# Differential attention heads in a hybrid decoder layer: merging maxima and sums by tensor_reduce, leaving head outputs in PSUM until they are stored, and making the high halves on ScalarE

## The chip, the cores and the metric

The kernel runs on one core of a Trainium2 chip. A core has five engines that run side by side and meet only through semaphores: TensorE (PE, matmuls; its weight loads are listed apart as PEld), VectorE (DVE), ScalarE (ACT), GpSimd (POOL) and SyncE (SP), which here issues the DMAs. Matmul results land in PSUM, a small memory of eight banks; everything else is held in SBUF. Each engine works through its own instructions strictly in order, so an instruction that waits holds up all that stands behind it.

The metric is device time in microseconds (us) of one execution, lower is better. Three executions of the kernel before took 2918.4 us (median), 2916.21 and 2920.43 us.

## The reference, cut to what matters

One decoder layer, sequence 2048, width 1024, float32 in and out:

```
h    = rmsnorm(x)
proj = h @ w_in                    # q, k, v of both head groups
8 heads x 64:  stick-breaking attention (sigmoids and a running product)
4 heads:       differential attention, two 64-wide maps each, 128-wide values:
    s[m] = (q[m] @ k[m].T) / 8, causal;  p[m] = softmax(s[m]),  m = 0, 1
    a    = p[0] - lam * p[1]
    o    = rmsnorm(a @ v) * (1 - lambda_init)          # per head
x = x + concat(heads) @ w_o
x = x + (silu(h2 @ w_gate) * (h2 @ w_up)) @ w_down     # h2 = rmsnorm(x)
```

q and k of the differential heads are also RMS-normed per 64 columns and rotated (rotary embedding).

Float32 accuracy is got from float16 matmuls: each operand is split into a high half (the value rounded to float16) and a low half (the rest), and a product is three matmuls, high by high, high by low and low by high.

## The kernel before, in words

**Stages.** The norm of the input with the first projections; the four pairs of stick-breaking heads; the four differential heads (g = 4 to 7); the output projection; the FFN. Projections of the next heads and, in the last head, the output projection of the first half, are cut into pieces and put between the attention work as filler for TensorE.

**Differential heads.** `units_diff` goes through 16 blocks of 128 queries ("rows" of a head, i = 0 to 15). Row i sees L = (i+1)*128 keys, in chunks of up to 1024. A unit is one map m (1 first, then 0) and one chunk j. A row therefore has two units when i < 8 (n = 1 chunk) and four when i >= 8 (n = 2). Of a unit, `scores` puts q by k into one of three two-bank PSUM slots; `front` takes the row maximum on DVE (L863, recorded through the helper `big` at L178) and, for the second chunk, merges it with that of the first (L865); `main` computes the bias (ACT, L871) and the exponentials with their sum (ACT, L874), both from PSUM.

**After the last unit of a row**, its remaining steps are put on a tick clock, one tick per unit: `coefs` (sums of two chunks added, L893, then a reciprocal and a product), `mix` (p0 plus a coefficient times p1, DVE, L178), `high` (float16 copy `ah`: ACT at L915 for rows with two chunks, DVE at L917 for the others) and `low` (the rest `al`: DVE, or POOL at L925 for one chunk of the long rows), each followed by a DMA transpose into `wt` (SP, L292). Then `values` at tick 7+n (PE: `wt` by v, three matmuls per 128 keys, into a 128-column PSUM place `acc`), `copy` at 8+n (ACT: acc to SBUF tile `on`, L946; squares with their sum, L948), `power` at 9+n (POOL), `store_high` at 10+n (ACT, L961) and `store` at 11+n (DVE, L966, then a DMA transpose, L968, and one tick later a DMA to `mix_d`, L710).

**The order inside a tick** is fixed by the main loop at the end of the attention part: first "ev" work, then `front` of unit n+1, then untagged work (`store`, `copy`), then `main` of unit n, then "mid" work (`values`, evacuations of projections), then the rest ("hi" work and `mix`, `low`), then the scores of unit n+2 and a piece of filler.

**PSUM.** It is one tile of 8 banks of 512 columns. In the differential stage `place` gives z (scores) banks 0 to 5 and `pj` (filler projections) the first 256 columns of bank 6 or 7 in turn; `av1`, the place of `acc`, is 128 columns in the upper half of the bank that the last `pj` tile did not get. Ordering between engines is put in by the framework, which orders accesses to the same bank.

**Projections of the differential heads** (`project_diff`): q and k parts are evacuated by ACT to `st` (L589); v by DVE, high at L605, low at L606. The rotation (`squares` to `finish`) is spread over some nine ticks on POOL and DVE; at its end `high` makes float16 copies of q (DVE, L665) and k (ACT, L666), and `finish` copies q's high half once more (DVE, L679). The helper `halved` makes a high half on ACT (L508) and a low half on DVE (L509) of a PSUM place.

Of the kernel before, what the change touches and what calls it, by code (L numbers as in the profile page):

```python
# [64 lines left out]
def hybrid_layer_kernel(  # L65
# [159 lines left out]
    with ExitStack() as actx:  # L225
# [24 lines left out]
        def place(kind, w):  # L250
            if kind == "av1":

                turn[kind] = 128 - turn.get(kind, 0)
                n = turn[kind] + (3840 if turn["pj"] % 2 == 0 else 3328)
                return psum[:, n:n + w]
            ps = places[mode[0]][kind]
            n = turn[kind] = (turn.get(kind, -1) + 1) % len(ps)
            return psum[:, ps[n]:ps[n] + w]


# [302 lines left out]
        def project_diff(c, g):  # L563
# [17 lines left out]
            for j in range(4):  # L581
# [21 lines left out]
                def evac_v(j=j, ps=ps):  # L603
                    vh, vl = v[:, j - 1:j + 1, 0, :], v[:, j - 1:j + 1, 1, :]
                    nc.vector.tensor_scalar(vh, ps, OUT_SC, None, ALU.mult)  # L605
                    nc.vector.scalar_tensor_tensor(vl, ps, OUT_SC, vh, ALU.mult, ALU.subtract)  # L606
# [54 lines left out]
            def high():  # L661
# [3 lines left out]
                nc.vector.tensor_copy(r["nq"][:, :, :, 0, :], xq)  # L665
# [11 lines left out]
            def finish():  # L677
                nq, nq2 = r["nq"], halves(n3)
                nc.vector.tensor_copy(nq2[:, :, :, 1, :], nq[:, :, :, 0, :])  # L679
# [152 lines left out]
        def unit_diff(g, i, m, j, cx):  # L832
# [21 lines left out]
            def front():  # L854

                if m == 1 and j == 0:
                    cx["mx"] = small("mx", 4, bufs=3)
                    cx["nb"] = small("nb", 4, bufs=3)
                    cx["su"] = small("su", 4, bufs=3)
# [4 lines left out]
                if j > 0:  # L864
                    nc.vector.tensor_max(mx[:, m:m + 1], mx[:, jj:jj + 1], mx[:, m:m + 1])  # L865

            def main():
                mx, nb, su = cx["mx"], cx["nb"], cx["su"]
                jj = 2 * j + m
                if j == 0:  # L870
                    nc.scalar.activation(nb[:, m:m + 1], mx[:, m:m + 1], AF.Identity,  # L871
                                         scale=nds_sc, bias=lnk)
# [16 lines left out]
            def coefs():  # L889
                su, cf = cx["su"], cx["cf"]  # L890
                steps = []
                if n == 2:
                    steps.append(lambda: nc.vector.tensor_add(su[:, 0:2], su[:, 0:2], su[:, 2:4]))  # L893
                steps += [lambda: nc.vector.reciprocal(cf[:, 0:1], su[:, 1:2]),
                          lambda: nc.vector.tensor_scalar(cf[:, 1:2], cf[:, 0:1], su[:, 0:1], nlam,
                                                          ALU.mult, ALU.mult)]

                def eps():
                    nc.gpsimd.tensor_scalar(cf[:, 2:3], su[:, 0:1], su[:, 0:1], scl[g][:, 2:3],
# [10 lines left out]
            def high(jc):  # L910
# [3 lines left out]
                if n == 2:  # L914
                    nc.scalar.copy(wh, p0)  # L915
                else:
                    nc.vector.tensor_copy(wh, p0)  # L917
# [12 lines left out]
            def values():  # L930
                acc = cx["acc"] = place("av1", 128)
# [800 lines left out]
```

## Time and profile before

| | us |
|---|---|
| median of 3 executions | 2918.4 |
| lowest, highest | 2916.21, 2920.43 |
| the profiled execution: time, span of its core | 2919.95, 2918.2 |
| busy in the span: PE, DVE, ACT, POOL | 2559.5, 2321.2, 1537.5, 1460.1 |
| mean granted TensorE clock | 0.947 of full speed |

All durations come from the one profiled execution, counted in microseconds from the start of its span; the 1.75 us between its time and its span lie outside what the trace shows. A group in the profile is named by line, engine, operation and tiles (output <- inputs), with its count, busy time, mean in ns, and the idle time of the engine just before, with what ended it. L167 is the helper through which all matmuls go, and L178 the helper `big`; there the tiles tell which step it is.

### The profile page before, as it was taken

How to read it: one execution, taken by the hardware profiler on the slowest of the kernel's cores; microseconds unless marked ns; L12 is line 12 of the kernel's file. 1: busy time of each engine (PE TensorE's matmuls, PEld its weight loads, DVE VectorE, ACT ScalarE, POOL GpSimd, SP SyncE). 2: the span in 40 equal slices, each digit the busy share in tenths (PEclk: the TensorE clock that was granted, in tenths of full speed). 3: DMA queues.
4: the chain of work that ended last, by engine and by line, in shares of the span. 5: the costliest groups of instructions: out<-in, count | busy, mean ns of one | idle time of the engine just before them, and what ended most of it. 6: DMA issues, size and time to landing. Idle time of an engine off the chain costs nothing.

```text
span 2918.2 us, 50458 instructions
## 1 busy us (share of the span) xinstructions
PE 2559.5 (88%) x19628; PEld 1475.6 (51%) x19628; DVE 2321.2 (80%) x3639; ACT 1537.5 (53%) x2587; POOL 1460.1 (50%) x1131
## 2 busy tenths in 40 slices
PE   6868878888687787776998899999999999999999
PEld 4435444446576676665763344444444444444444
DVE  7787878878898899899747788889877776776776
ACT  5777777877555555555415454544443343343332
POOL 1344444546667577576115456555445454445442
PEclk9979989889798899988999999999999999999999
DMA  4466776776745565667866312221126422112111
GB/s 157 83 129 119 131 131 114 140 127 124 130 74 96 94 106 100 127 121 135 188 155 139 106 65 103 96 80 62 44 87 132 135 94 73 44 44 87 44 44 72
DMA packets 734240, 301.55 MB, mean 103 GB/s; under 512 B 618672, under 2 KB 713264, under 8 KB 734000
## 3 DMA queue, kind: packets, MB, share of 16 engines
q1 hardware_dynamic: 733856, 298.30, 45.6%
q8 instruction: 153, 2.51, 0.4%
q14 instruction: 87, 0.71, 0.1%
q0 software_dynamic: 144, 0.03, 0.0%
HBM read 127.34 MB, written 28.31 MB: 53 GB/s over the span
## 4 chain that ended last, share of the span: by engine, by line
PE 48%; DVE 22%; ACT 9%; DMA 7%; POOL 6%; issue 6%; SPq 1%; DVEq 0%; ACTq 0%; POOLq 0%
PE pw L167 33%; PE psum L167 15%; DMA wt<-wl 3%; DVE mx L178 2%; DVE fs L1316 2%; DVE wl L790 2%; DVE acc_a L1589 2%; DVE gp L761 2%; ACT be L756 2%; DVE pt L178 1%; ACT gp L757 1%; DVE hh L1368 1%; DVE be L764 1%; ACT wh L785 1%; ACT psum L758 1%
## 5 line engine op out<-in xcount | busy, mean ns | idle before, releaser
L167 PE MATMUL pw<-t,fs 128*128 128x512 f16 x3696 | 808.5, 381 | 13.3 <-ACT fs L1315 3.8
L167 PEld LDWEIGHTS <-fs 128*128 128x128 f16 x3696 | 360.5, 98 | 452.4 <-issue 13.9
L772 POOL TENSOR_TENSOR be<-be,gp 128x1024 f32<-128x1024 f32 (+1 forms) x160 | 323.1, 2019 | 363.6 <-DVE gp L769 177.7
L167 PE MATMUL pw<-acc_b,at 128*128 128x512 f16 x2112 | 465.5, 380 | 17.2 <-DVE cg L1514 6.3
L167 PE MATMUL psum<-k,q 64*128 64x512 f16 (+4 forms) x1600 | 293.0, 383 | 131.9 <-ACT pt L874 79.8
L167 PE MATMUL psum<-ws,h_hi 128*128 128x128 f16 x4096 | 378.9, 225 | 17.3 <-ACT psum L948 10.8
L167 PE MATMUL psum<-ws,h_lo 128*128 128x128 f16 x2048 | 367.7, 224 | 0.0
L167 PEld LDWEIGHTS <-h_hi 128*128 128x128 f16 x4096 | 328.8, 101 | 47.5 <-issue 35.4
L167 PEld LDWEIGHTS <-at 128*128 128x128 f16 x2112 | 206.1, 98 | 268.7 <-issue 24.9
L1517 POOL TENSOR_TENSOR cg<-cg,cu 128x512 f32<-128x512 f32 x88 | 111.9, 1272 | 360.9 <-ACT cg L1516 341.1
L1589 DVE SCALAR_TENSOR_TENSOR acc_a<-pw,isd,acc_a 128x512 f32<-128x512 f32 x352 | 248.6, 744 | 49.9 <-PE pw L167 49.5
L761 DVE TENSOR_TENSOR_SCAN gp<-gp,psum 128x256 f32<-128x256 f32 (+1 forms) x320 | 196.4, 655 | 114.8 <-ACT psum L758 112.9
L1315 ACT ACTIVATE fs<-acc_b,fst 128x512 f16<-128x512 f32 x264 | 175.9, 713 | 211.1 <-POOL acc_b L1304 145.1
L1316 DVE SCALAR_TENSOR_TENSOR fs<-acc_b,fst,fs 128x512 f16<-128x512 f32 x264 | 248.2, 980 | 34.0 <-ACT fs L1315 33.9
L1506 POOL TENSOR_TENSOR sc<-sc 128x512 f32<-128x512 f32 x132 | 219.3, 1678 | 88.9 <-ACT sc L1500 88.9
L167 PEld LDWEIGHTS <-q 64*128 64x128 f16 (+1 forms) x1600 | 95.8, 100 | 239.2 <-issue 116.4
L167 PE MATMUL psum<-wt,v 128*64 128x256 f16 x1728 | 138.8, 308 | 84.8 <-DMA wt<-wl 74.4
L1500 ACT COPY sc<-pw 128x512 f32<-128x512 f32 x176 | 100.1, 580 | 211.4 <-PE pw L167 185.2
L167 PEld LDWEIGHTS <-h_lo 128*128 128x128 f16 x2048 | 206.5, 101 | 0.0
L874 ACT ACTIVATE pt<-psum,nb,ds_sc 128x1024 f32<-128x1024 f32 (+4 forms) x192 | 182.8, 952 | 21.6 <-DVE pt L178 8.3
L178 DVE TENSOR_REDUCE mx<-psum 128x1 f32<-128x1024 f32 (+4 forms) x192 | 173.6, 904 | 22.3 <-PE psum L167 21.6
L790 DVE TENSOR_TENSOR wl<-be,wh 128x1024 f16<-128x1024 f32 (+1 forms) x160 | 186.8, 1168 | 0.9 <-DMA wt<-wl 0.8
(224 smaller groups left out, 4596.3 us busy)
## 6 DMA issues: line engine op xcount, KB each, us to landing
acc_b<-in_w_gate_dram SPq DMA_DIRECT2D x22, 1024.0 KB, 5.2
acc_b<-in_w_up_dram SPq DMA_DIRECT2D x22, 1024.0 KB, 7.5
acc_b<-in_w_down_dram SPq DMA_DIRECT2D x22, 1024.0 KB, 9.4
raw<-in_w_in_dram SPq DMA_DIRECT2D x24, 512.0 KB, 4.5
xt<-in_x_dram SPq DMA_DIRECT2D x16, 512.0 KB, 5.5
raw<-in_w_o_dram SPq DMA_DIRECT2D x16, 512.0 KB, 4.0
mt<-mix_d SPq DMA_DIRECT2D x32, 256.0 KB, 3.4
out_dram<-acc_a SPq DMA_DIRECT2D x16, 512.0 KB, 2.6
```

What stands on the lines that cost most here:

```text
L167: nc.tensor.matmul(ps, lhsT=lhsT, rhs=rhs, start=start, stop=stop)
L178: fn(*a, **k)
L761: nc.vector.tensor_tensor_scan(ga, ga, z[:, h, P:W][:, ::-1], 2.0 ** 14 if diag else cx[a][:, h, 0:1], ALU.mult, ALU.mult)
L772: nc.gpsimd.tensor_mul(b4, b4, gp[:, :, 1:P + 1].rearrange("p h (r n) -> p h r n", r=1).to_broadcast([128, 2, 2, P]))
L790: nc.vector.tensor_sub(wl, b2, u["wh"])
L874: nc.scalar.activation(pt, u["z"][:, 0:e - b], AF.Exp, scale=ds_sc, bias=nb[:, m:m + 1], accum_out=su[:, jj:jj + 1])
L1315: nc.scalar.activation(w[:, m, 0:4], src, AF.Copy, scale=sw)
L1316: nc.vector.scalar_tensor_tensor(w[:, m, 4:8], src, sw, w[:, m, 0:4], ALU.mult, ALU.subtract)
L1500: nc.scalar.copy(s[m], y[m])
L1506: nc.gpsimd.tensor_add(s[m], s[m], y[m])
L1517: nc.gpsimd.tensor_mul(g, g, u)
L1589: nc.vector.scalar_tensor_tensor(acc[:, i, hs], ps, pr.isd, acc[:, i, hs], ALU.mult, ALU.add)
```

## The change

Four edits, all in the differential heads:

- the merging of two chunks' maxima and of their sums is done by `tensor_reduce` over wider tiles `mx` and `su`, into columns of their own, where `tensor_max` and `tensor_add` worked in place;
- a head's output stays in PSUM: `copy` no longer copies it to SBUF (the squares are now written to the SBUF tile `on`, and only their sum is used), and `store_high` and `store` read `acc` in PSUM. A new function `out_place` gives the place: it keeps a list of outputs not yet stored and takes the 128 columns of the bank that are free; where neither is free it would evict one to SBUF. In the built program it never does so: no copy of an `acc` is in it;
- v's high half is made by `halved` on ACT; q's float16 copy and its second copy go from DVE to ACT;
- `ah` of rows with one chunk goes from DVE to ACT.

```diff
@@ place @@
-            if kind == "av1":
-                turn[kind] = 128 - turn.get(kind, 0)
-                n = turn[kind] + (3840 if turn["pj"] % 2 == 0 else 3328)
-                return psum[:, n:n + w]
+        outs = []
+        def out_place(cx):
+            b = 3840 if turn["pj"] % 2 == 0 else 3328
+            free = [n for n in (b, b + 128) if n not in [o[0] for o in outs]]
+            if not free:
+                o = next(o for o in outs if o[0] in (b, b + 128))
+                outs.remove(o)
+                on = onp.tile([128, 128], F32, tag="on", name="on")
+                nc.scalar.copy(on, o[1]["acc"])
+                o[1]["acc"] = on
+                free = [o[0]]
+            outs.append((free[0], cx))
+            return psum[:, free[0]:free[0] + 128]
@@ project_diff @@
                 def evac_v(j=j, ps=ps):
-                    vh, vl = v[:, j - 1:j + 1, 0, :], v[:, j - 1:j + 1, 1, :]
-                    nc.vector.tensor_scalar(vh, ps, OUT_SC, None, ALU.mult)
-                    nc.vector.scalar_tensor_tensor(vl, ps, OUT_SC, vh, ALU.mult, ALU.subtract)
+                    halved(ps, v[:, j - 1:j + 1, 0, :], v[:, j - 1:j + 1, 1, :])
...
-                nc.vector.tensor_copy(r["nq"][:, :, :, 0, :], xq)
+                nc.scalar.copy(r["nq"][:, :, :, 0, :], xq)
...
-                nc.vector.tensor_copy(nq2[:, :, :, 1, :], nq[:, :, :, 0, :])
+                nc.scalar.copy(nq2[:, :, :, 1, :], nq[:, :, :, 0, :])
@@ unit_diff @@
                 if j > 0:
-                    nc.vector.tensor_max(mx[:, m:m + 1], mx[:, jj:jj + 1], mx[:, m:m + 1])
+                    nc.vector.tensor_reduce(mx[:, 4 + m:5 + m], mx[:, m:4:2], axis=AX.X,
+                                            op=ALU.max)
...
                 if n == 2:
-                    steps.append(lambda: nc.vector.tensor_add(su[:, 0:2], su[:, 0:2], su[:, 2:4]))
+                    steps.append(lambda: nc.vector.tensor_reduce(
+                        su[:, 4:6], su[:, 0:4].rearrange("p (j m) -> p m j", m=2), axis=AX.X,
+                        op=ALU.add))
...
-                if n == 2:
-                    nc.scalar.copy(wh, p0)
-                else:
-                    nc.vector.tensor_copy(wh, p0)
+                nc.scalar.copy(wh, p0)
...
             def values():
-                acc = cx["acc"] = place("av1", 128)
+                acc = cx["acc"] = out_place(cx)
...
             def copy():
-                on = cx["on"] = onp.tile([128, 128], F32, tag="on", name="on")
-                nc.scalar.copy(on, cx["acc"])
+                on = onp.tile([128, 128], F32, tag="on", name="on")
                 ss = cx["ss"] = small("oss", bufs=4)
-                nc.scalar.activation(cx["acc"], cx["acc"], AF.Square, accum_out=ss)
+                nc.scalar.activation(on, cx["acc"], AF.Square, accum_out=ss)
...
             def store():
-                on, ss = cx["on"], cx["ss"]
+                on, ss = cx["acc"], cx["ss"]
...
+                outs[:] = [o for o in outs if o[1] is not cx]
```

**Where it moves instructions.** TensorE's instructions stand in the same order as before; what they wait for is different. At the start of `values` of row 12 in head 6 (the first matmul of `wt` by v into `acc`) TensorE's queue read before:

```order
L167 LDWEIGHTS h_lo
L167 MATMUL psum<-ws,h_lo 128x128
L167 LDWEIGHTS wt [waits DMAHW1_49]
L167 MATMUL psum<-v,wt 128x128 [waits Activation_49]
L167 LDWEIGHTS wt
L167 MATMUL psum<-v,wt 128x128
```

and now:

```order
L167 LDWEIGHTS h_lo
L167 MATMUL psum<-ws,h_lo 128x128
L167 LDWEIGHTS wt [waits DMAHW1_49]
L167 MATMUL psum<-v,wt 128x128 [waits DVE_49]
L167 LDWEIGHTS wt
L167 MATMUL psum<-v,wt 128x128
```

The first matmul waited for ScalarE (an earlier evacuation out of that bank) and now waits for VectorE: for the `store` of row 11, which the program puts into the same tick a few instructions earlier, and whose output lies in the same bank.

On VectorE the same tick read before (from the maximum of the next unit, over the merges of sum and maximum and the `store` at L966, to the next maximum):

```order
L178 TENSOR_REDUCE mx<-psum 128x1 [waits PE_49,Activation_49]
L893 TENSOR_TENSOR su<-su 128x2 [waits Activation_49]
L865 TENSOR_TENSOR mx<-mx 128x1 [waits DVE_49]
L966 SCALAR_TENSOR_TENSOR mxs<-on,oss,mxs 128x128 [waits DMAHW6_49,Activation_49]
L178 TENSOR_TENSOR al<-pt,ah 128x768 [waits DMAHW3_49,Activation_49]
L894 RECIPROCAL cf<-su 128x1 [waits DVE_49]
L605 TENSOR_SCALAR v<-psum 128x2x128 [waits PE_49]
L606 SCALAR_TENSOR_TENSOR v<-psum,v 128x2x128 [waits DVE_49]
L178 TENSOR_REDUCE mx<-psum 128x1 [waits PE_49]
```

and now:

```order
L178 TENSOR_REDUCE mx<-psum 128x1 [waits PE_49,Activation_49]
L905 TENSOR_REDUCE su<-su 128x2 [waits Activation_49]
L875 TENSOR_REDUCE mx<-mx 128x1 [waits DVE_49]
L977 SCALAR_TENSOR_TENSOR mxs<-psum,oss,mxs 128x128 [waits DMAHW6_49,Activation_49]
L178 TENSOR_TENSOR al<-pt,ah 128x768 [waits DMAHW3_49,Activation_49]
L909 RECIPROCAL cf<-su 128x1 [waits DVE_49]
L521 SCALAR_TENSOR_TENSOR v<-psum,v 128x2x128 [waits Activation_49]
L178 TENSOR_REDUCE mx<-psum 128x1 [waits PE_49]
```

The order is kept; the high half of v is gone from the queue, and its low half (L606, now L521) waits for ScalarE where it stood behind VectorE's own instruction.

On ScalarE, in that tick and the next, the exponentials (L874) were followed by `ah` and `copy`:

```order
L874 ACTIVATE pt,su<-psum,nb,ds_sc 128x1024 [waits Activation_49]
L915 CAST ah<-pt 128x1024 [waits DMAHW4_49]
L946 COPY on<-psum 128x128 [waits PE_49]
L948 ACTIVATE psum,oss<-psum 128x128
L666 CAST rt<-st 128x8x64 [waits DMAHW3_49,DMAHW2_49,Pool_49]
```

and the same stretch now reads:

```order
L885 ACTIVATE pt,su<-psum,nb,ds_sc 128x1024 [waits Activation_49]
L520 ACTIVATE v<-psum 128x2x128 [waits PE_49]
L929 CAST ah<-pt 128x1024 [waits DMAHW4_49]
L959 ACTIVATE on,oss<-psum 128x128 [waits PE_49]
L675 CAST rt<-st 128x8x64 [waits DMAHW3_49,DMAHW2_49,Pool_49]
L676 CAST rt<-st 128x8x64 [waits Pool_49]
```

The high half of v stands behind that tick's exponentials, the copy of `acc` is gone, and the casts of q and k (L675, L676) now both stand here.

More of the change, by code (lines that the diff above doesn't have):

```diff
@@ L856, in front @@
                 if m == 1 and j == 0:
-                    cx["mx"] = small("mx", 4, bufs=3)
-                    cx["nb"] = small("nb", 4, bufs=3)
-                    cx["su"] = small("su", 4, bufs=3)
+                    cx["mx"] = small("mx", 6, bufs=3)
+                    cx["nb"] = small("nb", 2, bufs=3)
+                    cx["su"] = small("su", 6, bufs=3)
                     cx["cf"] = small("cf", 4, bufs=8)
@@ L870, in main @@
                 if j == 0:
-                    nc.scalar.activation(nb[:, m:m + 1], mx[:, m:m + 1], AF.Identity,
-                                         scale=nds_sc, bias=lnk)
+                    top = mx[:, m:m + 1] if n == 1 else mx[:, 4 + m:5 + m]
+                    nc.scalar.activation(nb[:, m:m + 1], top, AF.Identity, scale=nds_sc, bias=lnk)
                 pt = ptile("pt")[:, 0:e - b]
@@ L891, in coefs @@
                 steps = []
+                su0, su1 = su[:, 0:1], su[:, 1:2]
                 if n == 2:
-                    steps.append(lambda: nc.vector.tensor_add(su[:, 0:2], su[:, 0:2], su[:, 2:4]))
-                steps += [lambda: nc.vector.reciprocal(cf[:, 0:1], su[:, 1:2]),
-                          lambda: nc.vector.tensor_scalar(cf[:, 1:2], cf[:, 0:1], su[:, 0:1], nlam,
+                    steps.append(lambda: nc.vector.tensor_reduce(
+                        su[:, 4:6], su[:, 0:4].rearrange("p (j m) -> p m j", m=2), axis=AX.X,
+                        op=ALU.add))
+                    su0, su1 = su[:, 4:5], su[:, 5:6]
+                steps += [lambda: nc.vector.reciprocal(cf[:, 0:1], su1),
+                          lambda: nc.vector.tensor_scalar(cf[:, 1:2], cf[:, 0:1], su0, nlam,
                                                           ALU.mult, ALU.mult)]
                 def eps():
-                    nc.gpsimd.tensor_scalar(cf[:, 2:3], su[:, 0:1], su[:, 0:1], scl[g][:, 2:3],
+                    nc.gpsimd.tensor_scalar(cf[:, 2:3], su0, su0, scl[g][:, 2:3],
                                             ALU.mult, ALU.mult)
@@ L963, in store @@
             def store():
-                on, ss = cx["on"], cx["ss"]
+                on, ss = cx["acc"], cx["ss"]
                 oh, st = cx["oh"][:, 0], cx["oh"][:, 1]
```

## The prediction

> **What bounds the kernel now.** I read the slices of the page first, then the busy times of the stage that the change touches, then who waits for whom in it.
>
> ```profile
> PE 2559.5 (88%) x19628; PEld 1475.6 (51%) x19628; DVE 2321.2 (80%) x3639; ACT 1537.5 (53%) x2587; POOL 1460.1 (50%) x1131
> PE   6868878888687787776998899999999999999999
> DVE  7787878878898899899747788889877776776776
> ...
> PEclk9979989889798899988999999999999999999999
> ```
>
> PE is the busiest over the span, but only by its second half: from slice 20 on (1460 us) it stands at 9. From slice 10 to 18, where the differential heads run, DVE stands at 8 and 9 and PE at 6 to 8. The busy times of the differential stage while filler projections last (720 to 1400 us) and of its end:
>
> ```profile
> 720.00:1400.00 680.00, 512.68 (x6484) 426.54 (x6482) 603.15 (x1007) 378.07 (x876) 451.32 (x429) 0.89 0.60 111
> 1400.00:1500.00 100.00, 97.06 (x966) 82.61 (x966) 69.50 (x124) 44.17 (x95) 24.18 (x29) 1.00 0.77 169
> ```
>
> The columns are PE, PEld, DVE, ACT and POOL busy, then the clock. In the first stretch DVE is busy 603 of 680 us (89%), PE 513, ACT 378: DVE paces it, with 77 us idle. In the last 100 us PE is busy 97, so relief of DVE is worth nothing there. But DVE does not hold the whole chain in the first stretch:
>
> ```profile
> by line: PE psum L167 11.0%; issue 10.9%; DVE mx L178 8.0%; DVE pt L178 5.1%; DMA wt<-al 3.3%; POOL al L925 2.9%; DMA q<-rt 2.6%; DMA q<-st 2.6%; DVE rt L645 2.5%; POOL qss L108 2.2%; DVE wl L790 2.0%; DVE mxs L966 2.0%; DVE st L637 2.0%; P
> ```
>
> This is the chain of waits inside 720 to 1400. PE, POOL, the transposes and "issue" hold a good part of it; of the groups that the change touches only the store (mxs, L966) is named. And the waits (whole span; us in total, times, the longest):
>
> ```profile
> ACT nb L871 <- DVE mx L865: 108.7, 53, 4.6
> ...
> PE psum L167 <- ACT pt L874: 79.8, 52, 5.6
> ...
> ACT on L946 <- DVE mxs L966: 24.4, 10, 3.9
> ```
>
> ACT waits for merged maxima, PE for ACT to free a score slot: both run behind DVE, and DVE runs behind nobody for long.
>
> **The change part by part: VectorE.**
>
> ```profile
> L966 DVE SCALAR_TENSOR_TENSOR mxs<-on,oss,mxs 128x128 f16<-128x128 f32 x64 | 34.1, 532 | 12.1 <-ACT mxs L961 11.3 <-issue 0.6
> L865 DVE TENSOR_TENSOR mx<-mx 128x1 f32<-128x1 f32 x64 | 19.8, 310 | 0.9
> L917 DVE CAST ah<-pt 128x128 f16<-128x128 f32 (+7 forms) x32 | 18.3, 571 | 3.6 <-DMA wt<-ah 3.6
> L769 DVE TENSOR_REDUCE gp<-gp 128x2 f32<-128x2 f32 x96 | 14.3, 149 | 0.0
> L818 DVE SCALAR_TENSOR_TENSOR mxs<-psum,mxs 128x256 f16<-128x256 f32 x32 | 13.3, 415 | 0.2
> L605 DVE TENSOR_SCALAR v<-psum 128x256 f16<-128x256 f32 x32 | 13.2, 412 | 1.8 <-PE psum L167 1.7
> L665 DVE CAST rt<-st 128x512 f16<-128x512 f32 x16 | 11.2, 703 | 0.0
> L893 DVE TENSOR_TENSOR su<-su 128x2 f32<-128x2 f32 x32 | 11.2, 350 | 0.3 <-ACT pt L874 0.3
> L679 DVE COPY st<-rt 128x512 f16<-128x512 f16 x16 | 8.0, 502 | 0.6
> ```
>
> Four groups leave DVE: 13.2 (v) + 11.2 and 8.0 (q) + 18.3 (ah) = 50.7 us. Two change form. The nearest row for a tiny reduce is L769 (149 ns): the maxima cost 64 x 0.149 = 9.5 for 19.8, the sums 32 x 0.149 = 4.8 for 11.2, so 10.3 + 6.4 = 16.7 saved. The bound on the other side is that the new forms cost what the old ones do, nothing saved; I take 149 ns, since two or four inputs differ little from its two. The store's two forms:
>
> ```profile
> L966 DVE SCALAR_TENSOR_TENSOR mxs<-on,oss,mxs x64: 327/351/1841, 834.0 to 1499.0; 128x128 f16<-128x128 f32 x64
> ...
> L818 DVE SCALAR_TENSOR_TENSOR mxs<-psum,mxs x32: 408/414/425, 108.4 to 816.3; 128x256 f16<-128x256 f32 x32
> ```
>
> From SBUF it took 351 ns in the middle but 1841 at worst, mean 532; out of PSUM, at twice the width, it never left 408 to 425. For 128 columns out of PSUM I bound it by 0.415 (the same instruction at 256) and by 0.27 (less 128 columns, at the 1.21 us that 1024 columns out of PSUM take at 1287.86 in a row below); I take 0.29, near the lower, as the row at 256 hardly spreads: 64 x 0.29 = 18.6, 15.5 saved, or 7.5 at the upper bound. VectorE's sum: 50.7 + 16.7 + 15.5 = 83 us, of which I count 79 inside 720 to 1400 (nine of 64 merges and eight stores fall into the PE-bound end, three evacuations of v before). Between its bounds it is 51 to 83.
>
> [...]
>
> **ScalarE** loses 64 copies and gains four groups:
>
> ```profile
> L946 ACT COPY on<-psum 128x128 f32<-128x128 f32 x64 | 16.8, 263 | 99.2 <-PE psum L167 71.9 <-DVE mxs L966 24.4 <-DVE wsw L140 2.8
> L589 ACT ACTIVATE st<-psum 128x256 f32<-128x256 f32 x64 | 24.1, 376 | 25.6 <-DMA q<-st 17.6 <-PE psum L167 8.0
> L666 ACT CAST rt<-st 128x512 f16<-128x512 f32 x16 | 9.9, 616 | 17.3 <-POOL st L649 17.3
> L915 ACT CAST ah<-pt 128x128 f16<-128x128 f32 (+7 forms) x64 | 54.1, 849 | 0.0
> ```
>
> v: 32 x 0.376 = 12.0; q: 32 x 0.616 = 19.7; ah: 32 at narrower mean width than L915's 849 ns, some 21; less 16.8: 36 us more, 378 to 414 of 680. ACT has room, but room is not order: a moved instruction stands behind what ACT has before it. For `ah` and q the readers come a tick later, so ACT's idle time hides them; without that cover each would cost its 0.6 us. For v it does not hide: the low half follows at once on DVE, while the high half stands behind that tick's exponentials. The first and the last place where that bites:
>
> ```profile
> 837.51 1.20 ACT L874 ACTIVATE pt<-psum,nb,ds_sc 128x1024 f32<-128x1024 f32 x1
> 837.71 0.42 DVE L605 TENSOR_SCALAR v<-psum 128x256 f16<-128x256 f32 x1
> ...
> 1341.54 1.10 ACT L874 ACTIVATE pt<-psum,nb,ds_sc 128x896 f32<-128x896 f32 x1
> 1342.10 0.42 DVE L605 TENSOR_SCALAR v<-psum 128x256 f16<-128x256 f32 x1 [0.48 <-PE psum L167]
> ```
>
> At 837.71 DVE is ready, ACT is free at 838.71, its high half ends at 839.09: DVE stands 1.4 us. In 12 of the 32 places it is so, together 15.6 us: what the move of v gains (13.2) it gives back.
>
> **TensorE's new wait.** `acc` is now read until `store`, and a tick's `values` may go into the same bank. By the program 39 of the 64 `values` wait for a `store` that the same tick put in. A row of 13 blocks, and the first and last rows that would wait, before the change:
>
> ```profile
> 839.64 1.25 DVE L966 SCALAR_TENSOR_TENSOR mxs<-on,oss,mxs 128x128 f16<-128x128 f32 x1
> 839.94 0.83 PE L167 MATMUL psum<-v,wt 128*128 128x128 f16 x12
> ...
> 1281.14 2.34 PE L167 MATMUL psum<-v,wt 128*128 128x128 f16 x39
> 1283.32 1.03 PE L167 MATMUL psum<-k,q 128*128 128x512 f16 x4
> 1284.87 0.82 DVE L966 SCALAR_TENSOR_TENSOR mxs<-on,oss,mxs 128x128 f16<-128x128 f32 x1
> 1285.61 1.47 DVE L178 TENSOR_TENSOR al<-pt,ah 128x768 f16<-128x768 f32 x1
> 1287.86 1.21 DVE L178 TENSOR_REDUCE mx<-psum 128x1 f32<-128x1024 f32 x1
> ...
> 1373.60 2.72 PE L167 MATMUL psum<-v,wt 128*128 128x128 f16 x24 [2.28 <-ACT psum L948]
> ...
> 1376.76 1.05 DVE L966 SCALAR_TENSOR_TENSOR mxs<-on,oss,mxs 128x128 f16<-128x128 f32 x1 [0.91 <-ACT mxs L961]
> ```
>
> At 1281.14 PE started 4.6 us before that store ended at 1285.69; now it must wait for it. Of the 39, 26 start before their store ends, by 102 us together. Behind the waiting matmul stand 38 more of its row, then the scores (1283.32), and for these DVE waits at 1287.86. Store end 1285.69 + 2.4 of `values` + 1.2 of scores = 1289.3, so DVE would idle 1.5 us. Done so for each of the 39 (0.0575 us a matmul of `values` and 0.2 to start, 0.22 and 0.3 for scores), 19 come out short, 24.5 us together; for the others DVE's work between hides it. Bounds: 0, if a shorter DVE queue brings the store forward by as much, and 102, if every wait of PE lands on DVE.
>
> **The sum.** DVE's queue: -79 + 15.6 + 24.5 = -39 us. That would be the gain if DVE paced all of the stage. It is busy 89% and the chain runs over POOL, DMA and PE for a good part; those do not get shorter. I keep half: 20 us. The profiled execution took 2919.95 (span 2918.2 and 1.75 around it), so 2900 for such a one, and 2898 against the median, which lies 1.6 lower.
>
> **The rivals.** (1) DVE paces everything, and the new waits vanish because they are not additive (a DVE that waits for ACT finds PE caught up): 79 us off, 2840. For it: ACT and PE wait for DVE (108.7 and 79.8) and not the reverse; against it: the chain. (2) Nothing measurable: relief and new waits cancel, or the rotation's chain (POOL, transposes of q) sets the pace; 2913 to 2924. For it: POOL qss, q<-rt and q<-st hold 7.4% of the stage between them. (3) Slower: PE's wait for the store decides. PE would stand 102 us more; the 79.8 us in which it now waits for score slots it would not wait twice, so 22 us net, 2940. It decides from the point where PE, delayed at `values`, delivers scores after DVE has run dry in most rows, not in 19 of 64. Against it: PE has 167 us idle in the stage.
>
> [...]
>
> **Chances.** Forecast 0.52 with its own range 2882 to 2912; rival 1 0.12, rival 2 0.15, rival 3 0.21. A measurement of this kernel can tell about 0.2% (5.8 us) from no change. So faster 0.64, same 0.15, slower 0.21. The range reaches half-way to rival 1 (2858) and most of the way to rival 3 (2932).
>
> **What would show it.** DVE busy in the stage down by 70 to 85 us, the stores near 0.29 us without a tail, merges near 0.15; a new PE wait for the store (near 100 us in sum, or less if DVE gains ground), a new DVE wait for v's high half near 15, ACT's wait for `on` gone. Wrong if the stage is shorter by as much as DVE's relief (the waits then cost nothing), or if PE's busy share of it falls while DVE's idle time before the maxima (L178) more than doubles.

## The result and the profile after

The changed kernel takes 2962.2 us (median of four executions, 2955.98 to 2967.83); the kernel before, timed beside it, 2919.4. The ratio is 1.0145, with a 95% interval of 1.0115 to 1.0176: **slower by 43 us**, where 2898 us and a range of 2858 to 2932 were predicted. The profiled execution took 2955.98 us (span 2954.2), 36 us more than that of before, and its numbers are used below. Times and ratios go by undisturbed executions; one profiled execution, that of `psum_only` below, was disturbed (3446 us at a mean granted clock of 0.736), so the trace of that run is not read.

The first view is the page's busy times and slices after:

```profile
PE 2560.0 (87%) x19628; PEld 1477.2 (50%) x19628; DVE 2258.9 (76%) x3543; ACT 1570.6 (53%) x2619; POOL 1445.7 (49%) x1131
...
PE   6868878788777677776899899989999999999999
...
DVE  7787878878776677787756788889877776777776
```

VectorE is busy 62 us less, ScalarE 33 us more, TensorE as before. In slices 10 to 18 VectorE fell from 8 and 9 to 6 and 7 (one 8), and the two 8s of TensorE became 7s: the work is the same or less, and the idle time is new. Two windows of the run after; the first is the stage, the second begins after the attention and is as long as 1550 to 2918 of before:

```profile
720.00:1400.00 680.00, 487.16 (x6241) 408.58 (x6239) 516.27 (x865) 392.63 (x872) 421.36 (x411) 0.88 0.56 103
...
1586.00:2954.00 1368.00, 1323.73 (x6390) 599.29 (x6388) 1061.18 (x1467) 570.45 (x855) 662.33 (x479) 0.99 0.26 80
```

Before, that last stretch reads:

```profile
1550.00:2918.00 1368.00, 1321.03 (x6386) 598.04 (x6384) 1061.42 (x1467) 570.28 (x855) 661.50 (x478) 0.99 0.26 80
```

The same number of VectorE instructions fits into it, so the 36 us were lost before it, between 720 and the end of the attention. In 720 to 1400 TensorE is busy 487 us where it was 513, and it did 6241 matmuls where it did 6484: less of the stage fits in.

The groups on VectorE after (line, tiles, count, busy, mean ns, idle before and what ended it):

```profile
L178 DVE TENSOR_REDUCE mx<-psum 128x1 f32<-128x1024 f32 (+4 forms) x192 | 174.1, 907 | 76.9 <-PE psum L167 69.4 <-ACT ah L929 3.8 <-ACT st L601 1.9
L178 DVE SCALAR_TENSOR_TENSOR pt<-pt,cf 128x128 f32<-128x128 f32 (+7 forms) x96 | 107.0, 1116 | 0.0
L977 DVE SCALAR_TENSOR_TENSOR mxs<-psum,oss,mxs 128x128 f16<-128x128 f32 x64 | 22.1, 346 | 33.9 <-ACT mxs L972 12.4 <-issue 9.8 <-ACT pt L885 6.9
L521 DVE SCALAR_TENSOR_TENSOR v<-psum,v 128x256 f16<-128x256 f32 x29 | 12.2, 421 | 23.4 <-ACT v L520 23.4
L875 DVE TENSOR_REDUCE mx<-mx 128x1 f32<-128x2 f32 x64 | 9.9, 155 | 0.9
L905 DVE TENSOR_REDUCE su<-su 128x2 f32<-128x4 f32 x32 | 4.7, 146 | 0.7 <-ACT pt L885 0.7
```

and the first of them before:

```profile
L178 DVE TENSOR_REDUCE mx<-psum 128x1 f32<-128x1024 f32 (+4 forms) x192 | 173.6, 904 | 22.3 <-PE psum L167 21.6
L178 DVE SCALAR_TENSOR_TENSOR pt<-pt,cf 128x128 f32<-128x128 f32 (+7 forms) x96 | 103.1, 1076 | 0.0
```

The merges cost about what was predicted for them (149 ns), the store more (346 ns, where 290 was predicted). What grew is the idle time: before the maxima from 22.3 to 76.9 us, before v's low half from 2.8 (L605 and L606 of before: 1.8 + 1.0) to 23.4, before the store from 12.1 to 33.9. That is 97 us more idle, against 63 us less busy in this part (603 + 86 before, in 720 to 1400 and 1400 to 1550; 516 + 110 after, the second window 36 us longer): 34 us net, and 36 is what the span grew by. This is the account of one engine, not yet a cause. The waits of TensorE behind it (whole span; us in total, times, the longest):

```profile
PE psum L167 <- DVE mxs L977: 82.7, 27, 9.4
...
PE psum L167 <- ACT pt L885: 49.1, 27, 5.3
PE psum L167 <- ACT mxs L972: 32.9, 15, 7.0
```

TensorE stands 116 us for `store` (L977) and `store_high` (L972), where it never waited for either before; its wait for free score slots fell only from 79.8 to 49.1. Its waits for squares (L948, now L959; 18.8 to 1.0) and for transposes of `al` (22.7 to 6.1) fell too; together these give back 65 of the 116 us, and TensorE's idle time in the whole span grew by 36 us.

One place shows how. It is the same tick of the same row (33 matmuls, row 10 of head 4), right after the rotation's transposes of q. Before:

```profile
918.86 1.22 DVE L629 TENSOR_REDUCE qss<-rt 128x16 f32<-128x1024 f32 x1 [3.89 <-POOL rt L625]
919.74 0.38 ACT L589 ACTIVATE st<-psum 128x256 f32<-128x256 f32 x1 [6.03 <-DMA q<-st]
920.17 3.53 PE L167 MATMUL psum<-v,wt 128*128 128x128 f16 x33 [2.55 <-ACT st L589]
921.48 0.35 DVE L966 SCALAR_TENSOR_TENSOR mxs<-on,oss,mxs 128x128 f16<-128x128 f32 x1
...
924.61 1.22 DVE L178 TENSOR_REDUCE mx<-psum 128x1 f32<-128x1024 f32 x1 [0.98 <-PE psum L167]
```

and after:

```profile
923.39 0.38 ACT L601 ACTIVATE st<-psum 128x256 f32<-128x256 f32 x1 [6.25 <-DMA q<-st]
923.67 0.36 ACT L972 ACTIVATE mxs<-psum,oss 128x128 f16<-128x128 f32 x1
...
924.39 1.22 DVE L639 TENSOR_REDUCE qss<-rt 128x16 f32<-128x1024 f32 x1 [7.45 <-POOL rt L635]
...
927.01 0.35 DVE L977 SCALAR_TENSOR_TENSOR mxs<-psum,oss,mxs 128x128 f16<-128x128 f32 x1
...
927.41 3.68 PE L167 MATMUL psum<-v,wt 128*128 128x128 f16 x33 [7.55 <-DVE mxs L977]
...
932.72 1.23 DVE L178 TENSOR_REDUCE mx<-psum 128x1 f32<-128x1024 f32 x1 [3.57 <-PE psum L167]
```

In both, ScalarE stands some six us for the transposes, and VectorE four to seven. Before, `values` started 0.4 us after ScalarE's wait ended (919.74 to 920.17) and ran beside VectorE's backlog. Now it starts behind that backlog: the reduction of the rotation, the maximum, two merges and the store, 4.0 us after ScalarE's wait ended. The scores stand behind `values`, and VectorE, its backlog done, stands 3.57 us for them where it stood 0.98. At this place the stall went round: VectorE's delay became TensorE's, and TensorE's came back to VectorE.

The second kind of place is a filler matmul in a bank whose output is still held:

```profile
1331.50 2.91 POOL L108 TENSOR_TENSOR qss<-qss,mhalf 128x16 f32<-128x16 f32 x1 [2.00 <-DVE qss L641]
...
1334.40 3.18 POOL L914 TENSOR_SCALAR cf<-su,gsc 128x1 f32<-128x1 f32 x1
...
1338.61 0.37 ACT L972 ACTIVATE mxs<-psum,oss 128x128 f16<-128x128 f32 x1 [1.84 <-POOL oss L108]
...
1339.03 0.37 PE L167 MATMUL psum<-ws,h_hi 128*128 128x128 f16 x2 [7.00 <-ACT mxs L972]
```

`store_high` needs the root that GpSimd works out, and GpSimd is busy with the rotation (1331.50) and with a coefficient of another row (1334.40); TensorE stands 7.00 us for it with a matmul that has nothing to do with that row. Of the 15 waits for `store_high` all are at filler; of the 27 for `store` 26 are at `values`.

### The profile page after: what moved, and what is told of

The parts are those of the page before. It is cut to its first block, busy times and chain, and to the rows that moved or that the text cites. A ratio compares the mean times of both kernels' runs of the same rounds, so it can differ in the third digit from the quotient of the medians.

```text
span 2954.2 us, 50354 instructions
## 1 busy us (share of the span) xinstructions
PE 2560.0 (87%) x19628; PEld 1477.2 (50%) x19628; DVE 2258.9 (76%) x3543; ACT 1570.6 (53%) x2619; POOL 1445.7 (49%) x1131
## 4 chain that ended last, share of the span: by engine, by line
PE 37%; DVE 9%; ACT 3%; POOL 3%; issue 2%; DMA 1%; SPq 0%; ACTq 0%; DVEq 0%; POOLq 0%
PE pw L167 33%; PE psum L167 4%; DVE fs L1328 2%; DVE acc_a L1601 2%; DVE hh L1380 1%; POOL sc L1518 1%; DVE wmx L105 1%; ACT fs L1327 0%; DVE at L1534 0%; DVE cg L1526 0%; ACT pw L1370 0%; POOL hn L1366 0%; DVE fmx L105 0%; DMA t<-hh 0%; DVE acc_b L1576 0%
## 5 line engine op out<-in xcount | busy, mean ns | idle before, releaser
L178 DVE TENSOR_REDUCE mx<-psum 128x1 f32<-128x1024 f32 (+4 forms) x192 | 174.1, 907 | 76.9 <-PE psum L167 69.4
L167 PE MATMUL psum<-v,wt 128*128 128x128 f16 x1632 | 125.0, 244 | 88.0 <-DVE mxs L977 81.8
```

What stands on the lines that cost most here:

```text
L167: nc.tensor.matmul(ps, lhsT=lhsT, rhs=rhs, start=start, stop=stop)
L178: fn(*a, **k)
```

## The experiments

Times are medians; "+" is against the kernel before timed beside it, and the ratio with its 95% interval goes by the same runs.

**Which edit costs it.** The PSUM edit alone; everything but the PSUM edit; the same with v's high half back on VectorE; the two `tensor_reduce` merges alone.

`psum_only` is the kernel before with the diff's lines of `out_place`, `values`, `copy`, `store_high` and `store`, and nothing else of it:

```diff
...
-                nc.scalar.copy(on, cx["acc"])
...
-                on, ss = cx["on"], cx["ss"]
+                on, ss = cx["acc"], cx["ss"]
```

> Of the four edits only the outputs that stay in PSUM; maxima, sums, v, q and ah as before. Theory A (bank: TensorE waits for VectorE's store and ScalarE's store_high, which now read the bank that it wants to write): slower than before by 40 to 90 us, 2960 to 3010, with PE waiting for the store (L966 here) 80 us or more. Theory B (the work moved to ScalarE costs the time): within 10 us of before, or faster by up to 15 since the stores get shorter.

Measured: 2968.5 us, 1.017 [1.0151, 1.0189], +48, in the range of theory A.

`no_psum` is the change with those lines taken out again:

```diff
-                acc = cx["acc"] = out_place(cx)
+                acc = cx["acc"] = place("av1", 128)
...
-                on, ss = cx["acc"], cx["ss"]
+                on, ss = cx["on"], cx["ss"]
```

> The change without the outputs in PSUM: copy to SBUF and in-place squares as before, the other three edits made. Theory A: faster than before by 20 to 60 us, 2860 to 2900, since VectorE loses some 60 us and TensorE gets no new wait. Theory B: 2940 to 2965, slower than before, because the waits of VectorE for ScalarE's high half of v (31 us in the change) and ScalarE's longer queue remain.

Measured: 2924.9 us, 1.0015 [1.0005, 1.0025], +4: between the two ranges, so neither theory's figure held.

`no_psum_no_v` gives v's high half back to VectorE as well:

```diff
-                    halved(ps, v[:, j - 1:j + 1, 0, :], v[:, j - 1:j + 1, 1, :])
+                    nc.vector.tensor_scalar(vh, ps, OUT_SC, None, ALU.mult)
+                    nc.vector.scalar_tensor_tensor(vl, ps, OUT_SC, vh, ALU.mult, ALU.subtract)
```

> As the run without the outputs in PSUM, and v's high half back on VectorE. If the high half of v on ScalarE is a loss (theory B, or the prediction's sum of 13.2 us gained for 15.6 us waited), this is 0 to 20 us faster than that run; if it is a gain, 5 to 15 us slower.

Measured: 2925.1 us, 1.0007 [0.9994, 1.0021]: the same as `no_psum`.

`reduces_only` is the kernel before with the `tensor_reduce` merges of the diff only:

```diff
-                    nc.vector.tensor_max(mx[:, m:m + 1], mx[:, jj:jj + 1], mx[:, m:m + 1])
+                    nc.vector.tensor_reduce(mx[:, 4 + m:5 + m], mx[:, m:4:2], axis=AX.X,
+                                            op=ALU.max)
...
```

> The kernel before with the two merges by tensor_reduce alone: VectorE loses some 17 us, ScalarE gets nothing. If relief of VectorE is worth the third of its size that cutting mix showed (22 of 75): 4 to 8 us faster than before. If the whole of the three VectorE edits is worth nothing because relief at those places is: 0 within 3 us.

Measured: 2921.0 us, 1.0004 [0.9995, 1.0013]. Its trace shows why so little came of it. The merges of before had a long tail:

```profile
L865 DVE TENSOR_TENSOR mx<-mx x64: 146/159/2127, 841.6 to 1467.9; 128x1 f32<-128x1 f32 x64
```

In the middle they took 159 ns, hardly more than the 155 of the new form; the mean of 310 came from a few long ones, and these end together with an instruction of GpSimd, as here:

```profile
1049.04 2.13 POOL L925 TENSOR_TENSOR al<-pt,ah 128x1024 f16<-128x1024 f32 x1
1049.06 2.13 DVE L865 TENSOR_TENSOR mx<-mx 128x1 f32<-128x1 f32 x1
```

Of the 19 merges of before that took over 0.3 us, 17 end within 0.15 us of the end of a GpSimd instruction. The new merges never take over 157 ns, but `mix` got dearer in the same run:

```profile
L178 DVE SCALAR_TENSOR_TENSOR pt<-pt,cf 128x128 f32<-128x128 f32 (+7 forms) x96 | 111.5, 1163 | 0.0
```

That is 8.4 us more than before, and VectorE's busy time fell by 4 us (2321.2 to 2317.0) where the two groups had lost 17. At their middles the old merges come to 15 us of their 31, so most of what they gave up was that tail, not work; half as much came back at `mix`.

So the PSUM edit is the whole loss, and the other three edits, which took 53 us off VectorE, gained nothing. The busy times of `no_psum`:

```profile
PE 2569.0 (88%) x19628; PEld 1483.9 (51%) x19628; DVE 2268.5 (78%) x3543; ACT 1580.5 (54%) x2683; POOL 1461.5 (50%) x1131
```

Where most of the gain went shows in its groups, from 720 us to the end of the attention:

```profile
L178 DVE TENSOR_REDUCE mx<-psum 128x1 f32<-128x1024 f32 (+4 forms) x192 | 173.7, 905 | 38.5 <-PE psum L167 31.3 <-ACT ah L917 3.8 <-ACT st L589 1.7
L178 DVE SCALAR_TENSOR_TENSOR pt<-pt,cf 128x128 f32<-128x128 f32 (+7 forms) x96 | 110.7, 1155 | 0.0
...
L509 DVE SCALAR_TENSOR_TENSOR v<-psum,v 128x256 f16<-128x256 f32 x29 | 12.2, 419 | 21.2 <-ACT v L508 21.2
```

VectorE idles 18 us more for v's high half and 16 more before the maxima, and `mix` takes 8 us more (1155 ns where it was 1076). With v on VectorE again the time is the same, so the v edit is worth nothing either way.

**Bank or read?** The edit does two things: it reads the output out of PSUM, and it keeps the bank occupied. `high_in_psum` is `psum_only` with the SBUF copy kept for the store; only `store_high` reads PSUM:

```diff
                 nc.scalar.activation(on, cx["acc"], AF.Square, accum_out=ss)
+                nc.scalar.copy(on, cx["acc"])
...
             def store():
-                on, ss = cx["acc"], cx["ss"]
+                on, ss = cx["on"], cx["ss"]
```

> Only the outputs in PSUM, and only half of that: store_high on ScalarE reads the bank, store on VectorE reads an SBUF copy as before (the squares go to the copy's tile first). TensorE then waits for no store. If the wait for VectorE's store is what costs the 48 us of the run with the outputs in PSUM alone: 0 to 20 us slower than before, 2920 to 2940. If every holding of the bank costs alike: 30 to 50 slower, 2950 to 2970.

Measured: 2942.4 us, 1.0071 [1.0047, 1.0096], +21, just above the first range: not quite half the price, for a hold that ends one tick earlier. TensorE waits in it for no store, but for `store_high` much longer than in the change:

```profile
PE psum L167 <- ACT mxs L973: 69.3, 32, 7.0
```

Half of these waits are at `values` (16 times, 32 us) and half at filler (16 times, 37 us).

`z2_before` gives up one of the three score slots and puts the outputs into banks 6 and 7 in turn, without filler; `z2_psum` has the PSUM edit on top.

```diff
...
-            "diff": {"z": [0, 1024, 2048], "pj": [3072, 3584]}}
+            "diff": {"z": [0, 1024], "pj": [2048, 2560]}}
...
-                n = turn[kind] + (3840 if turn["pj"] % 2 == 0 else 3328)
+                n = turn[kind] = 3072 if turn.get(kind) == 3584 else 3584
```

> The kernel before with the PSUM banks shared out differently in the differential stage: two score slots (banks 0 to 3) in place of three, filler projections in banks 4 and 5, and the outputs of the heads in banks 6 and 7 in turn, where no filler comes; the outputs are still copied to SBUF. It is the control for the next run. With a slot less the scores of unit n+2 must wait for the exponentials of unit n, so all theories expect it slower than before, 2930 to 3010 us.

> The same places for the banks, and the outputs are left in PSUM until the store, as in the PSUM edit alone (which cost 48 us with three score slots and shared banks). Successive rows now write different banks and no filler shares them, so values waits only for the store of two rows before. Theory A (bank sharing is the price: TensorE's queue stands at the first matmul that goes to a bank whose held output is still read): no more than 10 us above its control, either side, and the waits of TensorE for mxs (L972 and L977 in the change, 33 and 83 us) all but gone. Theory B (reading the output out of PSUM twice more is itself dear, for ScalarE and VectorE, whatever the bank): 30 to 50 us above the control again.

Measured: 2985.9 us (1.0225 [1.0208, 1.0242]) and 2989.0 us (1.0235 [1.0215, 1.0254]). With a bank for itself the edit costs 3 us, within the noise of the two, where it cost 48. The waits of `z2_psum`:

```profile
PE psum L167 <- ACT pt L879: 165.1, 82, 5.0
...
PE psum L167 <- DVE mxs L970: 18.0, 13, 3.5
```

and its store:

```profile
L970 DVE SCALAR_TENSOR_TENSOR mxs<-psum,oss,mxs 128x128 f16<-128x128 f32 x64 | 21.8, 341 | 1.5 <-ACT mxs L965 1.5
```

TensorE waits 18 us for a store, and never for `store_high`; VectorE stands 1.5 us before its stores, not 33.9. Theory A holds: **the price is the sharing of the bank, not the reads out of it.** One reservation: with two score slots TensorE waits 165 us for ScalarE to free one, so a wait has more room to hide there; but most of the waits are gone, not hidden. The missing slot costs 64 us, so this is no way out. Outputs apart from the filler with three score slots (filler in bank 6 alone, outputs in bank 7) was not run, so what the edit costs there is not shown.

**Would another order give it back?** Four runs move one side of a wait.

`scores_first`: `values` behind the scores of unit n+2, so that no score stands behind its wait.

```diff
-                    clock.at(7 + n, values, "mid")
+                    clock.at(7 + n, values, "late")
...
             look_ahead(n)
+            clock.run("late")
```

> The whole change, but values is put behind the scores of unit n+2 in its tick, so that a TensorE that waits for the store holds up filler alone and no scores. Theory A in the form of the prediction (the wait starves VectorE of scores): 20 to 45 us faster than the change, 2915 to 2940, and VectorE's idle time before the maxima falls from 77 to under 40 us. If the wait costs TensorE's own throughput or ScalarE's order: no more than 10 us faster than the change.

Measured: 2955.2 us, 1.012 [1.0105, 1.0135].

`square_after`: the squares behind that tick's exponentials on ScalarE; `both_later`: this and `scores_first`; `no_psum_square`: this in `no_psum`, as control.

```diff
-                    clock.at(8 + n, copy, "")
+                    clock.at(8 + n, copy, "mid")
```

> The whole change, with copy (the squares, which wait for values) moved in its tick from ahead of the exponentials of unit n to behind them. Theory F (the loss is a ring: VectorE's store holds TensorE's values, these hold ScalarE's squares, and behind the squares stand the exponentials and, on GpSimd, the rest): 20 to 40 us faster than the change, 2920 to 2940, and PE's wait for exponentials and DVE's wait for scores fall. If the loss is TensorE's waiting as such: within 8 us of the change.

> The whole change, with values behind the scores of its tick and the squares behind the exponentials: a TensorE that waits for the bank holds up neither scores nor exponentials. Theory F: 2912 to 2930, nearly all of the 43 us back. Otherwise no better than the better of the two alone, 2945 to 2955.

> The change without the outputs in PSUM, copy and squares behind the exponentials of their tick. ScalarE waits 47 us for values and stores before that copy in the run without this move; if those waits hold up exponentials: 5 to 20 us faster than before, 2900 to 2915. If they fall into time that ScalarE has anyway: within 5 us of before, 2916 to 2926.

Measured: 2957.9 us, 1.0136 [1.0122, 1.015]; 2948.7 us, 1.0106 [1.0092, 1.012]; 2928.6 us, 1.004 [1.0025, 1.0056].

`store_later`: the store of rows with two chunks a tick later, so that `values` of that tick need not wait for it.

```diff
-                    clock.at(11 + n, store, "")
+                    clock.at((12 if n == 2 else 11) + n, store, "")
```

> The whole change, with the store of rows of two chunks one tick later, behind the next row's values instead of just ahead of it in the same tick: the 19 or so waits of values for a store in those rows go, those of the short rows stay. If the wait for the store is the cost: 15 to 30 us faster than the change, 2930 to 2945. If it is not: within 8 us of it, 2954 to 2966.

Measured: 2968.9 us, 1.016 [1.014, 1.018].

`scores_first` and `square_after` gave back 13 of 43 us together, so Theory F, the ring over ScalarE's squares, is refuted as the main cause; `store_later` nothing; without the PSUM edit the later squares cost 5 us (2928.6 against 2924.9, outside both ranges of that expectation). In `store_later` TensorE's waits for the store did fall, from 82.7 us in 27 places to 37.5 in 17, while those for `store_high` rose to 50.1 and those for score slots to 74.7. What moves is which wait bears the loss. The stage and two waits of `scores_first` (that window alone):

```profile
720.00:1400.00 680.00, 498.83 (x6316) 415.85 (x6316) 525.88 (x878) 399.28 (x887) 437.72 (x417) 0.88 0.56 104
```

```profile
PE psum L168 <- ACT pt L886: 76.3, 41, 6.1
...
PE psum L168 <- DVE mxs L978: 37.3, 18, 5.9
PE psum L168 <- ACT mxs L973: 33.6, 17, 6.2
DVE mx L179 <- PE psum L168: 22.7, 25, 2.9
```

VectorE's idle time before the maxima is down at 22.7 us in this window (58.8 in the change, 18.3 before), which is what the edit aimed at, and still the run is 35 us slower than before: TensorE stands for score slots and for `store_high` instead. VectorE's idle time moved as well, to 45.9 us before the stores and 35.2 before v's low half. So VectorE running dry of scores explains a small part of the loss at most.

**What paces the stage.** Three runs take work off one engine of the kernel before, and leave out part of the computation to do so.

`dve_less`: `mix` on an eighth of its columns; the second map is left out of the others.

```diff
-                big(nc.vector.scalar_tensor_tensor, p0, p1, cx["cf"][:, 1:2], p0, ALU.mult, ALU.add)
+                e8 = p0.shape[-1] // 8
+                big(nc.vector.scalar_tensor_tensor, p0[:, 0:e8], p1[:, 0:e8], cx["cf"][:, 1:2],
+                    p0[:, 0:e8], ALU.mult, ALU.add)
```

> The kernel before, with mix done on an eighth of its columns (the weights of the other columns then lack the second map): VectorE loses some 75 us in the differential stage, no other engine gets or loses work. Theory C (VectorE paces the stage, and the change's relief was taken back by ScalarE's longer queue): 2850 to 2885. Theory D (VectorE, though 89% busy, does not pace it): 2905 to 2925, no gain to speak of.

`pe_less`: the third product, low by high, of the differential projections left out.

```diff
-                    mm3(ps, h_hi[:, kk, ts], h_lo[:, kk, ts], ws[t][:, 0, kk, :],
-                        ws[t][:, 1, kk, :], kk == 0, kk == KB - 1)
+                    mm(ps, h_hi[:, kk, ts], ws[t][:, 0, kk, :], kk == 0, False)
+                    mm(ps, h_hi[:, kk, ts], ws[t][:, 1, kk, :], False, kk == KB - 1)
+                    pe[0] += 128
```

> The kernel before, with the product of the low half of h by the high half of the weights left out of the projections of the differential heads: 2048 of their 6144 matmuls, some 115 us of TensorE, nothing on the other engines; the planner still counts them, so the order of all else is kept. Theory E (TensorE's queue, its work and the waits it meets in order, is the length of the stage): 60 to 115 us faster, 2805 to 2860. Theory C (VectorE paces): less than 25 us faster.

`pool_less`: the gains of q and k left out.

```diff
-                nc.gpsimd.tensor_mul(y, y, qkg[:, t:t + 1, :].to_broadcast([128, 8, 64]))
```

> The kernel before without the multiplication of normalised q and k by their gains on GpSimd (L639; 32 instructions, 45.8 us, in 16 chains of rotation): the result is another one. Theory C (the chain of the rotation over GpSimd and the transposes of q paces the stage, as the second rival had it): 20 to 45 us faster. Theory D (no single engine's work paces the stage, each holds the path for a while): 0 to 12 us faster, like the 115 us that were taken off TensorE and gave 6 us.

Measured: 2899.2 us (0.992 [0.9898, 0.9942], -22), 2916.3 us (0.9979 [0.9967, 0.9992], -5) and 2904.6 us (0.9945 [0.9932, 0.9958], -17). The busy times of the three, in that order:

```profile
PE 2560.8 (88%) x19628; PEld 1473.9 (51%) x19628; DVE 2254.7 (78%) x3639; ACT 1537.8 (53%) x2587; POOL 1430.2 (49%) x1131
```

```profile
PE 2509.2 (86%) x18092; PEld 1409.7 (48%) x18092; DVE 2320.2 (80%) x3639; ACT 1536.8 (53%) x2587; POOL 1462.4 (50%) x1131
```

```profile
PE 2565.3 (88%) x19628; PEld 1479.4 (51%) x19628; DVE 2303.3 (79%) x3639; ACT 1537.2 (53%) x2587; POOL 1411.8 (49%) x1099
```

66 us off VectorE gave 22, 48 off GpSimd 17, 50 off TensorE 5. (Two expectations speak of 2048 matmuls and 115 us for TensorE: it was 1536, by their count, and 50 us of busy time.) The first and the third lie between the ranges that were expected. None of the three took from one engine alone. GpSimd is 30 us less busy in `dve_less` and VectorE 18 us in `pool_less`, with instructions that were not touched. And in `pe_less` the granted clock of the stage is 0.85, where it was 0.89:

```profile
720.00:1400.00 680.00, 470.71 (x5192) 371.20 (x5191) 608.29 (x1013) 381.04 (x880) 458.96 (x431) 0.85 0.59 112
```

The matmuls that are left took longer (those of `psum<-k,q` 393 ns in the mean over the span, 383 before). About a third of what is taken off VectorE or GpSimd comes out, other effects included, though VectorE is busy 89% of the stage and GpSimd 66% (451 of 680); Theory D is the nearer one, with GpSimd holding more of the path than it allowed. No run of this study beats the kernel before with the whole computation in it.

## Why the prediction was wrong, step by step

- **In the terms of its sum.** Of the -39 us the PSUM edit had some +10 (shorter stores -14, TensorE's wait +24.5) and the other three edits some -50 (-65, and +15.6 for v); halved, +5 and -25. Run one at a time they came to +48 and +4. Both terms failed, and the first by more.
- **The busy time of VectorE: right by rows, smaller in sum.** The merges cost 155 and 146 ns (149 predicted). The store cost 346 ns, not 290: midway between its bounds of 270 and 415, and its tail is gone, as predicted (326 to 352 ns against up to 1841). By groups 79 us left VectorE, against 83 in the sum; busy time fell by 63. Half of the rest is other groups that got dearer (8 us net, `mix` 4 of them); that the remainder is time in which neighbouring instructions had overlapped, counted twice in a group's sum, is inferred from the difference (the store at 1284.87 in the prediction's rows ends 0.08 us after the next instruction starts). And **the merges' term was mis-sized**: it took means of 310 and 350 ns for work, where the middle was 159 and 152 and the rest the tail above, up to 2127 and 2090. Of its 16.7 us `reduces_only` shows 4 in VectorE's busy time and none in the time.
- **v's high half: mechanism right, size short.** 15.6 us of VectorE's idle time were predicted, 18 (`no_psum`) to 21 (the change) measured. The edit was called worth about nothing, and was.
- **TensorE's new wait: right in size, wrong in what it costs.** Of 39 `values` 26 were to be late, by 102 us; 26 were, by 82 us (whether in the same rows is not shown). But **the step that carried this wait over to VectorE failed**: TensorE's wait was to cost only where it leaves VectorE without scores, 24.5 us before the maxima, and 55 came. It moved each `values` alone, in a timetable otherwise that of before, and so let VectorE's work stay where it was; and VectorE stood 22 us more before the stores, for which the sum had nothing. Nor is VectorE's wait for scores the whole way by which the time is lost: `scores_first` took 36 us of it away in the stage and gave back 8. That a late row makes VectorE late, this the next store, and that the next `values`, is seen at 927.41; how much of the loss this ring makes is not shown.
- **The fillers were left out of the sum.** **`store_high` holding up a filler matmul had no term**: 15 times, 32.9 us. A wait between two places of one bank stands in the prediction's rows: 2.28 us at 1373.60 for the squares (L948) of the row before, which by the program lie in other columns than the place that `values` writes. Rival 3 was priced without such waits. In the change a filler matmul stands 7.00 us for `store_high` (1339.03 above), and the two-slot pair gives the price of the sharing as a whole: 48 us where banks are shared (three slots), 3 where not (two slots).
- **"VectorE paces it, half of its relief counts": failed.** The three other edits took 53 us off VectorE and gave nothing (+4 us). `dve_less` got a third, from `mix`, which later steps of the row wait for, and with GpSimd 30 us less busy as well. The 89% in the window were read as a bound; the chain of waits quoted under it, with no line above 11% of the stage, was the better witness.
- **The rivals.** Rival 3 is what happened, at 2962 where it had 2940. Its netting was wrong: TensorE's waits for score slots fell by 31 us, not by all of the 79.8, and the fillers' waits were missing; that its size came near the measured one is in part luck. Its condition, VectorE dry of scores in most rows, came about (40 waits in the stage, 16 before), but `scores_first` shows that this is not what the loss hangs on. Rival 1 was refuted by `no_psum`, and rival 2 holds for the other three edits taken alone. The sign that was to refute the forecast came about as written: TensorE's busy share of the stage fell (513 to 487 of 680), and VectorE's idle time before the maxima more than doubled (22 to 77).
- **Slips that change nothing.** The bounds of VectorE's relief come to 58 and 84 us by the terms given (51 to 83 in the text), 2858 is two thirds of the way to rival 1, and the 79.8 us under rival 1 are TensorE's waits for ScalarE, not for VectorE.
- **Still open** is how the 48 us divide between `values` behind `store` and fillers behind `store_high`, and by which path they reach the end. `high_in_psum` does not separate them, as half of its waits for `store_high` are at `values`. Nor is a wait's length its price: with TensorE's waits for the two at 116 us in the change, 88 in `store_later`, 77 in `scores_first` and 69 in `high_in_psum`, the loss is 43, 48, 35 and 21 us (the first three runs have the other three edits in them).

## What to carry to other kernels

Before a result is left in PSUM to save a copy, list every instruction of TensorE that goes to the same bank until the last reader is done, and for each what that reader is queued behind: here a 0.26 us copy on ScalarE was what had kept TensorE from waiting for `store` and `store_high` (no wait before, 116 us after). An engine that is busy 89% of a stage is not thereby what paces it; taking some work off it in a dummy run, before its relief is put into a sum, tells how much of the relief comes out, if the other engines' busy times and the granted clock are read with it. Where a group's mean lies far above its middle, the difference may be waiting, which can come back at another instruction when the first is made cheaper (here 310 ns against 159 for the maxima; `mix` rose by 8.4 us). And a new wait between engines that already wait for each other should not be priced place by place in the old timetable: here that gave 24.5 us, and the edit cost 48.

## What the runs showed of the hardware that was not expected

- The 128-column reads out of PSUM cost no more than those from SBUF: the store 350 ns in the middle against 351, `store_high` 363 in the mean against 394. The two forms of each differ in the number of SBUF inputs as well, so what the source alone costs is not shown.
- With work taken off VectorE an instruction that stayed on it took longer in these runs: `mix`, from SBUF to SBUF on 96 places, took 1076 ns before, 1116 after and 1155 in `no_psum`, 4 and 8 us in sum (in `z2_psum`, with shorter stores, it did not: 1052, against 1101 in `z2_before`). What holds it is not shown; the rows point to GpSimd. The merges' tail (up to 2127 ns, where the middle was 159) ended with GpSimd's instructions 17 times in 19, it was gone once a merge read one input instead of two (157 ns at most), and `mix` got 8.4 us dearer in that run. In `reduces_only` 28 of the 92 mixes that the timeline shows singly are over 0.15 us longer than the shortest of their width, 18 us together (before: 21 of 90, 9 us), and in 27 of the 28 (before: in all 21) a GpSimd instruction ended about where that shortest time would have begun.
- The busy times of the two engines fell together, both ways: with `mix` cut to an eighth GpSimd was 30 us less busy on the same instructions (1460.1 to 1430.2), and with the gains left out of GpSimd VectorE was 18 us less busy (2321.2 to 2303.3).
- With matmuls left out the granted clock was lower: 5192 matmuls in 680 us of the stage at 0.85 in `pe_less`, 6484 at 0.89 before; over the span 0.934 to 0.940 in its ten executions, 0.941 to 0.951 in the 13 of before beside them. 1536 matmuls fewer took only 50 us off TensorE's busy time.
